# A decoder trunk in fp32 on one core: spare matmuls at the start, the first input chunk loaded first, and a last norm whose sums enter the root as its scale and bias

## The chip, the cores and the metric

The kernel runs on one core of a Trainium2 chip. The metric is device time in microseconds (us) of one execution; less is better. Three runs of the kernel before gave 1189.68, 1192.73 and 1192.95 us, a median of 1192.73. The profile and the trace come from a fourth, profiled execution.

A core has engines that run their own instruction streams and wait for each other by semaphores: TensorE (PE, with its weight loads as PEld), VectorE (DVE), ScalarE (ACT), GpSimd (POOL) and SyncE (SP). SP, POOL and ACT also start DMA transfers; each of these rows stands in the queue of the engine that issues it.

## What is computed

The input is x (512 tokens of 1024 numbers, float32). Two layers follow each other, an SGU mixer and a retention mixer, each with a SwiGLU feed-forward behind it; every block has an RMS norm in front and a residual add behind, and one RMS norm ends the trunk:

```python
def rmsnorm(x, g):
    xf = x.astype(jnp.float32)
    y = xf * lax.rsqrt(jnp.mean(xf * xf, axis=-1, keepdims=True) + EPS)
    return (y * g.astype(jnp.float32)).astype(x.dtype)
...
    h = x
    for i in range(DEPTH):
        hn = rmsnorm(h, mix_norm_g[i])
        j = i // N_MIXERS
        if i % N_MIXERS == 0:
            h = h + sgu_mixer(hn, sgu_w_in[j], sgu_w_s[j], sgu_b_s[j],
                              sgu_ln_g[j], sgu_ln_b[j], sgu_w_out[j])
        else:
            h = h + retention(hn, positions, ret_w_in[j], ret_gn_g[j], ret_w_out[j])
        h = h + swiglu(rmsnorm(h, ffn_norm_g[i]), ffn_w_gu[i], ffn_w_down[i])
    return rmsnorm(h, final_norm_g)
```

The change touches two ends of this: the first products of the SGU mixer, those of the half `v` of `gelu(h @ w_in)`, and the last line.

## The kernel before

The tokens are worked on in four chunks (`NC`) of 128, the partitions of a tile. Every fp32 product is made of three products of fp32r halves: a matrix is split into a high half (a copy on ACT: `wh`, `XH`) and a low half (the difference, on DVE: `wl`, `XL`), and PE adds up wh·XH, wl·XH and wh·XL. Most of the large products after the first also use sums of blocks in the manner of Strassen (`seven`, L836); they fill the middle of the span and are not touched.

No instruction is issued where it stands in the code. A `Recorder` (L211) takes each call down as an operation with its engine, the tiles that it reads and writes, and an estimate of its duration (`record`, L285). `order_of` (L423) then plans: `deadlines` goes back from the end and gives each operation a latest time, `forward` (L462) goes through the time from the start and gives each engine, whenever it is free, the operation whose inputs are there and whose latest time is nearest; it also models the DMA queues, each with its issue time by engine (SP 450, POOL 1200, ACT 100 in the planner's units) and a landing time, and grants buffers. `emit` (L619) writes the operations in this order to the engines' streams. The order on an engine is then fixed: an instruction whose input is late holds up all that stand behind it on that engine. Since everything goes through the recorder, nearly all rows of the profile carry one line, L337, and are told apart by the names of their tiles.

The start (L1342 to L1367): the rows of the first norm's gain go through a DMA of POOL (`load_rows`), X's first chunk and the first weight (`wr_v`) come on SP, in halves of 128x512 that the planner has put in turn: weight, X, weight, X. `rows_to_cols` turns the gain rows by a small matmul into `mix_ps`, which DVE copies into `mix_cols`. `turn_in(c)` (L1193) turns chunk c by eight transposes on PE into `xT_in`; ACT makes the high half `XH_in` in eight pieces, scaled by `mix_cols`; DVE makes `xr_in` and from it the low half `XL_in`, in two halves each. `square_in` (the tile `xq`) sums the squares of a chunk, for chunk 0 on DVE and for the others on ACT. `natural_step` (L820) adds the three products of two blocks of 128 rows into `ps_v`. Five small matmuls on a tile of ones, `wake` (ten instructions in the trace), stand ahead of all that on PE. `ones`, `eps` and the identity are made on POOL. Behind the products of `v`'s first half PE does `gains_ps`, the turned gains of the later norms.

The end: the last down product writes into X by blocks (`into_x`, L1031), and for each half (j) of a chunk (c) the last norm follows: `chunk_norm` (L1137) squares the half on ACT with a sum (`sq_dn`), `with_gain` (L1304) multiplies it by the gain `g_fin` on DVE for all but chunk 1's second half, and with the second half the two sums are added (`ss_dn`). `norm_factor` (L1161) makes 1/sqrt from the sum with a root on ACT, a reciprocal on DVE and a refinement step of three rows on DVE (all `nf_dn`); `finish` (L1313) scales the halves (`o`) on ACT, or on DVE for chunk 1, and sends each with a DMA, chunk 0's on ACT's queue and the others on SP's. Chunk 1's second half is the last to be ready.

## Time and profile before

| | |
|---|---|
| median of three runs | 1192.73 us (1189.68 to 1192.95) |
| profiled execution, its own time | 1187.3 us |
| its span in the trace | 1185.6 us |
| PE busy | 1168.7 us in 7494 matmul rows |
| ACT busy, DVE busy | 691.1 us, 999.5 us |
| first matmul (`wake`), first product of `ps_v` | 2.33 us, 8.77 us |
| PE's last matmul starts, last row on DVE starts | 1177.70 us, 1181.71 us |

The span is what the trace covers, 1.7 us less than the profiled execution's own time; the runs without a profile lie 2.4 to 5.7 us above that. A row of the timeline has a start and a duration in us, the engine, the line, the operation with output and inputs, the tile's shape, a count where equal rows follow each other, and in brackets how long the engine stood idle before it and what ended that. Matmuls are pipelined: the distance from one start to the next tells PE's pace better than a row's duration.

### The profile page before, as it was taken

To read this page: it belongs to the slowest core of one execution; us is meant where nothing else is said; L and a number is where in the kernel's file an instruction comes from. 1 tells how busy PE (TensorE), PEld (TensorE's weight loads), DVE (VectorE), ACT (ScalarE), POOL (GpSimd) and SP (SyncE) were. 2 spreads that over 40 slices of the span, in tenths; PEclk is the share of its full clock that TensorE was granted. 3 is DMA by queue.
4 is the path that set the end of the run, shared out by engine and by line. 5 is a ranking of instruction groups with operands and counts; after the bars stand their busy time and mean duration, and the time that the engine had idled before them with its cause. 6 is when DMAs were issued, how large, how long until landed. Compare 5 with 4: busy or idle time off the path is not lost.

```text
span 1185.6 us, 18730 instructions
## 1 busy us (share of the span) xinstructions
PE 1168.7 (99%) x7494; PEld 1064.7 (90%) x7494; DVE 999.5 (84%) x1168; ACT 691.1 (58%) x870; POOL 180.3 (15%) x159
## 2 busy tenths in 40 slices
PE   8999999999999999999999999999999999999997
PEld 6899899989999988888989898888899989999986
DVE  7998999897779799998968678899988896665895
ACT  7445776455443567756656575577675555435474
POOL 1002121211100120221111011220211111001220
PEclk9999999999999999999999999999999999999999
DMA  9349989798855888879667688698897798668891
GB/s 331 98 123 207 317 183 219 169 244 199 218 155 143 204 177 273 195 173 238 161 175 175 157 204 202 169 172 262 226 213 178 182 240 206 174 174 234 187 231 72
DMA packets 132808, 232.99 MB, mean 197 GB/s; under 512 B 7624, under 2 KB 32240, under 8 KB 132720
## 3 DMA queue, kind: packets, MB, share of 16 engines
q1 hardware_dynamic: 90928, 156.52, 40.4%
q0 software_dynamic: 41504, 74.74, 37.7%
q8 instruction: 59, 0.97, 0.3%
q10 hardware_dynamic: 288, 0.52, 0.1%
q14 instruction: 29, 0.24, 0.1%
HBM read 228.61 MB, written 2.10 MB: 195 GB/s over the span
## 4 chain that ended last, share of the span: by engine, by line
PE 89%; DVE 6%; DMA 3%; ACT 1%; issue 1%; DVEq 0%; ACTq 0%; SPq 0%; POOLq 0%
PE X_gu L337 21%; PE Y_gu L337 10%; PE X_dn L337 8%; PE X_vg L337 7%; PE Z_gu L337 5%; PE Y_dn L337 4%; PE X_qk L337 4%; PE Y_vg L337 4%; PE ps_v L337 4%; PE X_ro L337 3%; PE pv L337 2%; PE Y_qk L337 2%; PE X_so L337 2%; PE Y_ro L337 2%; PE Z_dn L337 2%; PE X_u L337 1%
## 5 line engine op out<-in xcount | busy, mean ns | idle before, releaser
L337 ACT ACTIVATE wh_gu_P<-wr_gu_P 128x1024 fp32r<-128x1024 f32 x132 | 137.4, 1055 | 124.2 <-DVE wr_gu_P L337 39.9
L337 DVE TENSOR_TENSOR wl_gu_P<-wr_gu_P,wh_gu_P 128x1024 fp32r<-128x1024 f32 x132 | 159.5, 1221 | 48.4 <-ACT wh_gu_P L337 39.9
L337 POOL DMA_DIRECT2D wr_gu_P<-in_ffn_w_gu x50 | 60.8, 1245 | 380.1 <-DVE wl_gu_P L337 161.3
L337 ACT ACTIVATE wh_dn_P<-wr_dn_P 128x1024 fp32r<-128x1024 f32 (+1 forms) x72 | 69.2, 981 | 44.4 <-PE Y_gu L337 9.5
L337 DVE TENSOR_TENSOR wl_dn_P<-wr_dn_P,wh_dn_P 128x1024 fp32r<-128x1024 f32 (+1 forms) x72 | 80.2, 1130 | 7.1 <-ACT wh_dn_P L337 6.5
L337 POOL DMA_DIRECT2D wr_dn_P<-in_ffn_w_down x40 | 46.4, 1202 | 173.0 <-DMA wr_dn_P<-in_ffn_w_down 66.9
L337 DVE TENSOR_TENSOR wl_vg_P<-wr_vg_P,wh_vg_P 128x1024 fp32r<-128x1024 f32 x48 | 57.4, 1219 | 8.7 <-ACT wh_vg_P L337 7.6
L337 ACT ACTIVATE wh_vg_P<-wr_vg_P 128x1024 fp32r<-128x1024 f32 x48 | 49.1, 1059 | 18.0 <-DMA wr_vg_P<-in_ret_w_in 9.5
L337 POOL DMA_DIRECT2D wr_vg_P<-in_ret_w_in x26 | 32.2, 1321 | 135.9 <-DVE wl_vg_P L337 61.4
L337 PE MATMUL X_gu<-xP3h_f,wh_gu_P 128*128 128x256 f32 x176 | 50.3, 286 | 0.0
L337 PE MATMUL X_gu<-xP5h_f,wh_gu_P 128*128 128x256 f32 x176 | 49.9, 284 | 0.3 <-ACT u L337 0.3
L337 PE MATMUL Z_gu<-XH_f,wh_gu_P 128*128 128x256 f32 x176 | 50.0, 284 | 0.0
L337 PE MATMUL X_gu<-XH_f,wh_gu_P 128*128 128x256 f32 x176 | 49.9, 284 | 0.0
L337 PE MATMUL Y_gu<-xP7l_f,wh_gu_P 128*128 128x256 f32 x176 | 49.8, 283 | 0.0
L337 PE MATMUL X_gu<-xP6h_f,wh_gu_P 128*128 128x256 f32 x176 | 49.8, 283 | 0.0
L337 PE MATMUL X_gu<-xP6l_f,wh_gu_P 128*128 128x256 f32 x176 | 49.8, 283 | 0.0
L337 PE MATMUL X_gu<-xP6h_f,wl_gu_P 128*128 128x256 f32 x176 | 49.8, 283 | 0.0
L337 PE MATMUL Y_gu<-XL_f,wh_gu_Q 128*128 128x256 f32 x176 | 49.8, 283 | 0.0
L337 PE MATMUL Y_gu<-XH_f,wl_gu_Q 128*128 128x256 f32 x176 | 49.8, 283 | 0.0
L337 PE MATMUL Y_gu<-xP7h_f,wl_gu_P 128*128 128x256 f32 x176 | 49.8, 283 | 0.0
L337 PE MATMUL Y_gu<-xP7h_f,wh_gu_P 128*128 128x256 f32 x176 | 49.8, 283 | 0.0
L337 PE MATMUL Y_gu<-XH_f,wh_gu_Q 128*128 128x256 f32 x176 | 49.8, 283 | 0.0
(675 smaller groups left out, 4377.8 us busy)
## 6 DMA issues: line engine op xcount, KB each, us to landing
wr_gu_P<-in_ffn_w_gu SPq DMA_DIRECT2D x110, 512.0 KB, 5.4
wr_gu_P<-in_ffn_w_gu POOLq DMA_DIRECT2D x50, 512.0 KB, 7.8
wr_dn_P<-in_ffn_w_down SPq DMA_DIRECT2D x50, 512.0 KB, 5.3
wr_vg_P<-in_ret_w_in SPq DMA_DIRECT2D x40, 512.0 KB, 5.2
wr_dn_P<-in_ffn_w_down POOLq DMA_DIRECT2D x33, 512.0 KB, 7.5
wr_vg_P<-in_ret_w_in POOLq DMA_DIRECT2D x26, 512.0 KB, 7.8
wr_qk_P<-in_ret_w_in SPq DMA_DIRECT2D x20, 512.0 KB, 4.7
wr_ro_P<-in_ret_w_out SPq DMA_DIRECT2D x20, 512.0 KB, 4.8
```

Of the source, the lines that this page charges most:

```text
L337: return fn(*[real_of(a) for a in args], **{k: real_of(a) for k, a in kwargs.items()})
```

## The change

At the start, 60 spare matmuls are offered to the planner: products of `onesr` with itself, 128 columns wide, into `vps[1]`, the second `ps_v` tile, which is overwritten later. `forward` puts one on PE wherever PE would have nothing to do between 2500 and 14000 of its time units, as long as that tile has not had its first product, and counts it with 120 units before 7000 and 60 behind; 52 are used. Before 7000 all PE operations count double. X's first chunk and the gain's rows get an earlier place (`rec.ahead`), so that X's two loads stand ahead of the first weight's on SP. Loads granted early are counted late by 600 instead of 1500, and a DMA issue on ACT costs 450 instead of 100. `ones` and `eps` are set on DVE.

At the end, the first half's sum becomes `base` = sum/D + EPS at once, and when the second half's sum s is there, the root is taken as sqrt(s/D + base) with 1/D as the activation's scale and `base` as its bias, without an add of the two sums (`norm_parts`). It gives r (the reciprocal of the root) and u (the refinement's factor) apart; chunk 1 is scaled by both at once, the others by their product z on ACT. All halves are multiplied by the gain beforehand, chunk 1's second half too; a chunk's second half is scaled and sent first, and only one of the eight outputs, chunk 1's first half, goes out on ACT's queue.

The order on PE at the start of the program, before the change (`xT_in` are the transposes of a chunk, `ps_v` the products):

```order
L337 MATMUL wake<-ones 128x128 x5
L337 MATMUL mix_ps<-ident,mix_rows 128x8
L337 MATMUL xT_in_123<-ident,X 128x128 x8
L337 MATMUL ps_v_0_147<-wh_v_0_115,XH_in 128x512
L337 MATMUL ps_v_0_147<-wl_v_0_126,XH_in 128x512
L337 MATMUL xT_in_158<-ident,X 128x128 x8
L337 MATMUL ps_v_0_147<-wh_v_0_115,XL_in 128x512
L337 MATMUL ps_v_0_147<-wh_v_0_115,XH_in 128x512
```

The same place of PE in the changed kernel, from behind `wake` (L1397 are the spares; `ps_v_1` is the tile that they write):

```order
L343 MATMUL mix_ps<-ident,mix_rows 128x8
L343 MATMUL xT_in_127<-ident,X 128x128 x5
L1397 MATMUL ps_v_1_110<-onesr 128x128 x5
L343 MATMUL ps_v_0_159<-wh_v_0_145,XH_in 128x512
L1397 MATMUL ps_v_1_110<-onesr 128x128
L343 MATMUL ps_v_0_159<-wl_v_0_155,XH_in 128x512
L1397 MATMUL ps_v_1_110<-onesr 128x128 x22
L343 MATMUL xT_in_201<-ident,X 128x128 x4
L1397 MATMUL ps_v_1_110<-onesr 128x128 x6
L343 MATMUL xT_in_201<-ident,X 128x128 x4
L1397 MATMUL ps_v_1_110<-onesr 128x128 x2
L343 MATMUL ps_v_0_159<-wh_v_0_145,XL_in 128x512
```

Twelve more spares, and three transposes of chunk 0, stand between `wake` and these rows. The transposes of chunk 0 now stand ahead of and behind `mix_ps`, and 30 spares with the eight transposes of chunk 1 lie between the second product of `ps_v` and the first with `XL_in`.

The order on ACT at the start, before (`wh_v` is the high half of a weight, `XH_in` that of a chunk):

```order
L337 ACTIVATE wh_v_0_115<-wr_v_0_80 128x512 x2
L337 ACTIVATE XH_in<-xT_in_123,mix_cols 128x128 x8
L337 ACTIVATE wh_v_1_161<-wr_v_1_100 128x1024
L337 ACTIVATE XH_in<-xT_in_158,mix_cols 128x128 x8
L337 ACTIVATE wh_v_2_198<-wr_v_2_109 128x1024
L337 ACTIVATE xq_209,ss_140<-X 128x1024
L337 ACTIVATE wh_v_3_225<-wr_v_3_117 128x1024
```

And the same place of ACT in the changed kernel:

```order
L343 ACTIVATE wh_v_0_145<-wr_v_0_94 128x512
L343 ACTIVATE XH_in<-xT_in_127,mix_cols 128x128 x8
L343 ACTIVATE wh_v_0_145<-wr_v_0_94 128x512
L343 ACTIVATE wh_v_1_194<-wr_v_1_104 128x1024
L343 ACTIVATE xq_216,ss_141<-X 128x1024
L343 ACTIVATE XH_in<-xT_in_201,mix_cols 128x128 x8
L343 ACTIVATE wh_v_2_254<-wr_v_2_117 128x1024
```

The second half of the first weight has moved behind `XH_in` of chunk 0, and the squares of a chunk (`xq`) have moved ahead of `XH_in` of chunk 1.

The order on DVE at the end of the program, before, from the last add into X on (`nf_dn_1_1` are the small tiles of chunk 1's norm, `o` the outputs):

```order
L337 TENSOR_TENSOR X<-X,W_dn_1_11799 128x512
L337 TENSOR_TENSOR ss_dn_1_11781<-ss_dn_1_11654 128x1
L337 TENSOR_SCALAR nf_dn_1_1_11875<-ss_dn_1_11781 128x1
L337 RECIPROCAL nf_dn_1_1_11877<-nf_dn_1_1_11873 128x1
L337 SCALAR_TENSOR_TENSOR nf_dn_1_1_11879<-nf_dn_1_1_11877,nf_dn_1_1_11875 128x1
L337 TENSOR_SCALAR nf_dn_1_1_11881<-nf_dn_1_1_11879 128x1
L337 TENSOR_TENSOR nf_dn_1_1_11883<-nf_dn_1_1_11881,nf_dn_1_1_11877 128x1
L337 TENSOR_SCALAR o_0_11722<-o_0_11722,nf_dn_1_1_11883 128x512
L337 SCALAR_TENSOR_TENSOR o_1_11886<-X,nf_dn_1_1_11883,g_fin 128x512
```

And the end of DVE's stream in the changed kernel:

```order
L343 TENSOR_TENSOR X<-X,W_dn_1_11858 128x512
L343 TENSOR_TENSOR o_1_11928<-X,g_fin 128x512
L343 TENSOR_SCALAR nf_dn_1_1_11932<-ss_dn_1_11704,nf_dn_1_1_11788 128x1
L343 RECIPROCAL nf_dn_1_1_11934<-nf_dn_1_1_11930 128x1
L343 SCALAR_TENSOR_TENSOR nf_dn_1_1_11936<-nf_dn_1_1_11934,nf_dn_1_1_11932 128x1
L343 TENSOR_SCALAR nf_dn_1_1_11938<-nf_dn_1_1_11936 128x1
L343 TENSOR_SCALAR o_1_11928<-o_1_11928,nf_dn_1_1_11938,nf_dn_1_1_11934 128x512
L343 TENSOR_SCALAR o_0_11791<-o_0_11791,nf_dn_1_1_11938,nf_dn_1_1_11934 128x512
```

The add of the sums and the last small multiply are gone, the product of the last half with the gain has moved ahead of the norm's small rows, and both scalings take two of them.

The diff, cut where it only passes the list of spares on:

```diff
--- before.py
+++ after.py
@@ -32,6 +32,7 @@
 SUM = 7
 N_GEN = 39
 N_TMP = 5
+SPARES = 60
 SO = ("P1", "P7", "P6", "Q4", "P5", "P2", "P3")
 UO = ("P1", "P7", "P6", "P2", "Q4", "P5", "P3")
 U_DMA = ("P7",)
...
@@ -253,6 +254,11 @@
         self.ops.append(op)
         return op
 
+    def spare(self, call, tile):
+        op = Op()
+        op.engine, op.call, op.what, op.tiles, op.n = "PE", call, "spare", [tile], 0
+        self.spares.append(op)
+
     def issue_after(self, ins):
         return nullcontext()
 
@@ -305,7 +311,7 @@
     if name == "dma_start":
         kind = "add" if "accum_op" in kwargs else "load" if writes else "store"
         size = n * 4 * (writes or reads)[0].shape[0]
-        busy = {"SP": 450, "POOL": 1200, "ACT": 100}[engine]
+        busy = {"SP": 450, "POOL": 1200, "ACT": 450}[engine]
         took = busy
         slow = max(60, size * (SERVE_ADD if kind == "add" else SERVE) // 524288)
     elif name == "transpose":
@@ -353,6 +359,12 @@
 BOTH = 0.95
 LATE = 1500
 ROUNDS = 1
+FILL_FROM = 2500
+FILL_TO = 14000
+WARM = 7000
+SPARE = 120
+EARLY_LOADS = 4000
+LATE_FIRST = 600
 SURE = 2000
 EARLY = False
 POOL_DATA = 640
@@ -431,21 +443,21 @@
-        end = forward(ops)
+        end, used = forward(ops, rec.spares)
...
-    return sorted(ops, key=lambda o: (o.start, o.n))
+    return sorted(ops + used, key=lambda o: (o.start, o.n))
...
@@ -512,8 +524,9 @@
             kind = min((k for k in lane if lane[k]), key=lambda k: lane[k][0][1] / rate(k))
             op = lane[kind].pop(0)[0]
             op.end = now
-            started(op, now + LATE)
-            post(now + LATE, op)
+            late = LATE if op.start > EARLY_LOADS else LATE_FIRST
+            started(op, now + late)
+            post(now + late, op)
         left = [max(0, q[0][1]) / rate(kind) for kind, q in lane.items() if q]
         if left:
             version += 1
@@ -531,6 +544,13 @@
     grant()
     finished = 0
     soon = {"DVE": [], "ACT": []}
+    used, left = [], spares[::-1]
+
+    def may_fill():
+        if not left or not FILL_FROM <= now < FILL_TO:
+            return False
+        t = left[-1].tiles[0]
+        return t.granted is not None and t.first.start is None
 
     def started(op, end):
         for q in op.after:
@@ -588,6 +608,13 @@
                             cost = o.late + (3 * TABLE if o.table and o.table != table else 0)
                             if op is None or (cost, o.n) < best:
                                 op, best = o, (cost, o.n)
+                if op is None and e == "PE" and may_fill():
+                    op = left.pop()
+                    used.append(op)
+                    op.start = now
+                    busy_until[e] = now + (SPARE if now < WARM else SPARE // 2)
+                    post(busy_until[e], None)
+                    continue
                 if op is None or e in soon and not op.kind and better(e, op):
                     break
                 queue[e].remove(op)
@@ -596,7 +623,7 @@
                     if q.left == 0:
                         queue["PE"].append(q)
                 op.start = now
-                held = op.busy
+                held = op.busy * 2 if e == "PE" and now < WARM else op.busy
                 if op.table and op.table != table:
                     table = op.table
                     held += TABLE
...
@@ -679,9 +706,9 @@
     ident = const.tile([P, P], F32, name="ident")
     rec.add("POOL", lambda: make_identity(rec.real, ident.realize()), [], [ident.view()], "identity", 600, 600)
     ones = const.tile([P, P], F32, name="ones")
-    nc.gpsimd.memset(ones, 1.0)
+    nc.vector.memset(ones, 1.0)
     eps = const.tile([P, 1], F32, name="eps")
-    nc.gpsimd.memset(eps, EPS)
+    nc.vector.memset(eps, EPS)
     onesr = const.tile([P, P], F32R, name="onesr")
     nc.vector.tensor_copy(onesr, ones)
     nc.scalar.activation(const.tile([P, 1], F32, name="first"), ones[:, 0:1], AF.Gelu_apprx_tanh)
@@ -1137,7 +1164,7 @@
     def chunk_norm(name, ready, half=None):
 
 
-        halves_of = [0] * NC
+        halves_of, first_half = [0] * NC, [None] * NC
         ss = small.tile([P, NC], F32, tag="ss", name=f"ss_{name}")
         part = small.tile([P, 2 * NC], F32, tag="ss0", name=f"ss0_{name}")
 
@@ -1153,10 +1180,27 @@
                     half(c, j)
                 halves_of[c] += 1
                 if halves_of[c] == 1:
+                    if half:
+                        base = small.tile([P, 1], F32, tag="nf16", name=f"nf6_{name}_{c}", bufs=4)
+                        nc.vector.tensor_scalar(base, both[:, j:j + 1], 1.0 / D, EPS, ALU.mult, ALU.add)
+                        first_half[c] = base
+                    return
+                if half:
+                    ready(c, norm_parts(both[:, j:j + 1], first_half[c], f"{name}_{c}"))
                     return
                 nc.vector.tensor_tensor(ss[:, c:c + 1], both[:, 0:1], both[:, 1:2], ALU.add)
             ready(c, norm_factor(ss[:, c:c + 1], D, f"{name}_{c}"))
         return norm
+
+    def norm_parts(ss, base, name):
+
+        a, root, r, t, u = (small.tile([P, 1], F32, tag=f"nf1{i}", name=f"nf{i}_{name}", bufs=4) for i in range(5))
+        nc.scalar.activation(root, ss, AF.Sqrt, scale=1.0 / D, bias=base)
+        nc.vector.tensor_scalar(a, ss, 1.0 / D, base, ALU.mult, ALU.add)
+        nc.vector.reciprocal(r, root)
+        nc.vector.scalar_tensor_tensor(t, r, a, r, ALU.mult, ALU.mult)
+        nc.vector.tensor_scalar(u, t, -0.5, 1.5, ALU.mult, ALU.add)
+        return r, u
 
     def norm_factor(ss, n, name):
 
@@ -1305,24 +1349,22 @@
 
         if not fin:
             fin.append(gain_tile("g_fin", fin_g[None, :]))
-        if (c, j) != (1, 1):
-            o = gained[c, j] = G(f"o{c}_{j}")[:, 0, :]
-            js = slice(j * T, (j + 1) * T)
-            nc.vector.tensor_tensor(o, X[:, c, js], fin[0][:, js], ALU.mult)
-
-    def finish(c, r):
-        for j in range(2):
-            js = slice(j * T, (j + 1) * T)
-            if (c, j) in gained:
-                o = gained[c, j]
-                if c == 1:
-                    nc.vector.tensor_scalar(o, o, r, None, ALU.mult)
-                else:
-                    nc.scalar.activation(o, o, AF.Copy, scale=r)
+        o = gained[c, j] = G(f"o{c}_{j}")[:, 0, :]
+        js = slice(j * T, (j + 1) * T)
+        nc.vector.tensor_tensor(o, X[:, c, js], fin[0][:, js], ALU.mult)
+
+    def finish(c, ru):
+        r, u = ru
+        if c != 1:
+            z = small.tile([P, 1], F32, tag="nf15", name=f"nf5_end_{c}", bufs=4)
+            nc.vector.tensor_tensor(z, u, r, ALU.mult)
+        for j in (1, 0):
+            o = gained[c, j]
+            if c == 1:
+                nc.vector.tensor_scalar(o, o, u, r, ALU.mult, ALU.mult)
             else:
-                o = TMP(f"o{c}_{j}")
-                nc.vector.scalar_tensor_tensor(o, X[:, c, js], r, fin[0][:, js], ALU.mult, ALU.mult)
-            (nc.scalar if c == 0 else nc.sync).dma_start(out[c * P:(c + 1) * P, js], o)
+                nc.scalar.activation(o, o, AF.Copy, scale=z)
+            (nc.scalar if (c, j) == (1, 0) else nc.sync).dma_start(out[c * P:(c + 1) * P, j * T:(j + 1) * T], o)
 
 
     ss2 = small.tile([P, NC], F32, tag="ss2", name="ss2", bufs=1)
@@ -1339,8 +1381,10 @@
         else:
             nc.scalar.activation(sq, X[:, c, :], AF.Square, accum_out=ss2[:, c:c + 1])
 
+    rec.ahead = 3000
     load_rows(nc.gpsimd, "mix0", mix_g[0:1])
     load_x(0)
+    rec.ahead = 0
     v0w = [None] * NC
     wr = G("wr_v0_0")
     for a in range(2):
@@ -1348,6 +1392,12 @@
     mix0 = rows_to_cols("mix0")
     turn_in(0)
     vps = [PS(f"ps_v0_{i}") for i in range(2)]
+
+    def keep_warm():
+        rec.real.tensor.matmul(vps[1][:, 0, 0:P].realize(), onesr.view().realize(), onesr.view().realize(), start=True, stop=True)
+
+    for _ in range(SPARES):
+        rec.spare(keep_warm, vps[1])
     for i in range(NC):
         if i > 0:
             wr = fetch_tile(f"v0_{i}", w_in, 2 * i, 2, ((D, T),))
```

More of the change, by code (lines that the diff above doesn't have):

```diff
@@ L215, in __init__ @@
         self.tc, self.real = tc, tc.nc
-        self.ops, self.held, self.ahead = [], {}, 0
+        self.ops, self.held, self.ahead, self.spares = [], {}, 0, []
         for attr in ENGINE_OF:
@@ L433, in order_of @@
         deadlines(ops, total)
-        end = forward(ops)
+        end, used = forward(ops, rec.spares)
         if best is None or end < best[0]:
-            best = end, [(o.start, o.end, o.late) for o in ops], [(t, t.granted, t.when) for o in ops for t in o.new]
+            best = end, [(o.start, o.end, o.late) for o in ops], [(t, t.granted, t.when) for o in ops for t in o.new], used
         total = end
@@ L440, in order_of @@
                 op.late = op.start
-    end, times, places = best
+    end, times, places, used = best
     for op, (op.start, op.end, op.late) in zip(ops, times):
@@ L459, in deadlines, with forward @@
     backward(ops, lazy, total, gap)
-def forward(ops):
+def forward(ops, spares):
     import heapq
@@ L615, in forward @@
                            f"{ {k[1]: (len(slots[k]), len(w)) for k, w in waiting.items() if w} }")
-    return now
+    return now, used
 def emit(rec):
```

## The prediction

> **What bounds the kernel now.** I read the page first (busy times, then the chain that ended last), then PE's waits behind the start, then the timeline of the first 36 us and of the last 8.
>
> ```profile
> PE 1168.7 (99%) x7494; PEld 1064.7 (90%) x7494; DVE 999.5 (84%) x1168; ACT 691.1 (58%) x870; POOL 180.3 (15%) x159
> PE 89%; DVE 6%; DMA 3%; ACT 1%; issue 1%; DVEq 0%; ACTq 0%; SPq 0%; POOLq 0%
> PE X_qk L337 <- ACT xP6h_r L337: 1.5, 1, 1.5
> ...
> PE X_gu L337 <- ACT u L337: 0.3, 1, 0.3
> ```
>
> PE works 99% of the 1185.6 us span and is 89% of the chain. The three rows below the chain are the first and the last of all seven waits that PE has after 12 us: 5.2 us together, none of them on a DMA. So almost any time that PE gains or loses at the start is passed on to the end, and only the start and the tail behind PE's last matmul can move. Those are the two places that the change touches; the order of the middle is the same but for two neighbouring weight loads on SP.
>
> The start, from the timeline (start, duration, what; in brackets the idle time before and its releaser):
>
> ```profile
> 0.81 0.39 SPq L337 DMA_DIRECT2D wr_v<-in_sgu_w_in  x1
> 2.04 0.24 POOL L337 MEMSET ones<- 128x128 f32 x1
> 2.33 2.50 PE L337 MATMUL wake<-ones 128*128 128x128 f32 x10 [2.33 <-POOL ones L337]
> 5.21 0.63 ACT L337 ACTIVATE wh_v<-wr_v 128x512 fp32r<-128x512 f32 x1 [2.70 <-DMA wr_v<-in_sgu_w_in]
> 6.12 0.24 PE L337 MATMUL mix_ps<-ident,mix_rows 8*128 8x8 f32 x1 [1.28 <-DMA mix_rows<-in_mix_norm_g]
> 6.40 0.17 DVE L337 COPY mix_cols<-mix_ps 128x8 f32<-128x8 f32 x1 [3.86 <-PE mix_ps L337]
> 6.54 0.63 ACT L337 ACTIVATE wh_v<-wr_v 128x512 fp32r<-128x512 f32 x1 [0.70 <-DMA wr_v<-in_sgu_w_in]
> 7.20 0.72 PEld L337 LDWEIGHTS xT_in<-ident,X 128*128 128x128 f32 x4 [0.19 <-DMA X<-in_x]
> 7.82 1.22 DVE L337 SCALAR_TENSOR_TENSOR xq<-X 128x1024 f32<-128x1024 f32 x1
> 8.35 2.18 ACT L337 ACTIVATE XH_in<-xT_in,mix_cols 128x128 fp32r<-128x128 f32 x8 [1.18 <-PE xT_in L337]
> 8.77 0.80 PE L337 MATMUL ps_v<-wh_v,XH_in 128*128 128x512 f32 x1 [0.46 <-ACT XH_in L337]
> 9.79 1.88 PE L337 MATMUL xT_in<-ident,X 128*128 128x128 f32 x8
> 11.29 0.69 DVE L337 TENSOR_TENSOR XL_in<-xr_in,XH_in 128x512 fp32r<-128x512 f32 x1
> 12.04 0.50 PE L337 MATMUL ps_v<-wh_v,XL_in 128*128 128x512 f32 x1 [0.36 <-DVE XL_in L337]
> 12.37 0.40 PE L337 MATMUL ps_v<-wh_v,XH_in 128*128 128x512 f32 x1
> 14.90 0.60 PE L337 MATMUL xT_in<-ident,X 128*128 128x128 f32 x4
> 15.39 0.50 PE L337 MATMUL ps_v<-wh_v,XL_in 128*128 128x512 f32 x1
> 21.46 1.03 PE L337 MATMUL xT_in<-ident,X 128*128 128x128 f32 x8
> 22.25 0.47 PE L337 MATMUL ps_v<-wh_v,XH_in 128*128 128x512 f32 x1
> 35.63 0.25 PE L337 MATMUL gains_ps<-ident,gains_rows 32*128 32x32 f32 x1
> ```
>
> Two things are to be seen. The first four transfers land one after the other, 0.65 us apart: first at 5.2, third at 6.54, fourth at 7.2, so the second at about 5.9. And PE has two speeds: eight transposes take 1.88 us at 9.79 (0.235 each), and 0.79 from 21.46 to 22.25 (0.1 each); a 512-column product takes 0.228 (the chain's row of 22.50, below). It became fast shortly before 12.04: 2.9 to 3.3 us after the work that began, with hardly a break, at 8.77, or 5.9 us after that of 6.12.
>
> **The start, changed.** X's two halves come first and land at 5.2 and 5.9; the memset of ones moves from POOL, where a DMA and its start-up stood ahead of it until 2.04, to DVE, where it is the first instruction: from 0.81, when SP begins, 0.24 later wake can begin, at 1.05 instead of 2.33. eps, the second, is wanted by nothing near the start. PE then has work without a break: wake, 12 spares, transposes. By 2.9 to 3.3 us of unbroken work it is fast at 4 to 4.4; by 5.9 at 7. I take the first, as the break at 4.83 to 6.12 in the old start speaks for a fresh count. The gains do not follow from X alone, though. mix_ps still waits for its rows until 6.12 (its DMA stays on POOL), and ACT's first wh_v now stands ahead of XH_in and takes the third landing: 6.54 + 0.63 = 7.2. So XH_in begins at 7.2 instead of 8.35 and its last input of chunk 0 (xr_in, half a wl_v, XL_in) is there at about 11.35 rather than 11.98 (8.35 to 11.98 is 3.6; plus 0.6 for the wl_v now between, less overlap).
>
> That 0.6 us is not what PE sees. DVE holds mix_cols (to 6.6), xq (1.22) and the first wl_v (0.69, the row of XL_in has the same size) ahead of the second product: it starts at 8.5 and ends at 8.7. Behind it the order puts 22 + 6 + 2 spares and the 8 transposes of chunk 1 ahead of the product with XL_in. What does a spare cost? It is a 128-column fp32r product, and the trace has such ones late in the retention layer:
>
> ```profile
> 609.60 0.26 PE L337 MATMUL sc<-q1h,k1h 128*128 128x128 f32 x1
> ...
> 610.26 0.44 PE L337 MATMUL Y_vg<-wh_vg_Q,XL_r 128*128 128x512 f32 x1
> 22.50 13.20 PE ps_v L337 x58
> 170.60 5.76 PE Z_gu L337 x48
> ```
>
> Six of them stand from 609.60 to 610.26: 0.11 each. (The last two rows, from the chain, give 0.228 for 512 columns and 0.12 for 256; a line through them would make 128 columns 0.066.) I take 0.11, the row of the same size. Then the XL_in product starts at 8.7 + 30 x 0.11 + 8 x 0.1 = 12.8, against 12.04: **+0.8**. The spares that were to fill idle time outlast it by 1.4 us, since the data is there at 11.35. Behind it stand four more spares between chunk 2's transposes, +0.4; against that, the slow first product of 12.04 (0.33 to the next, 0.1 over) and some 0.2 of the 14.90 to 15.39 stretch (four transposes in 0.49, where 21.46 gives 0.4, and a slow product behind) may go. Start: 0.8 + 0.4 - 0.3 = **+0.9**.
>
> Bounds: with spares at 0.066 the product with XL_in waits for its data at 11.35, the later chunks' XL_in (XH_in of chunk 1 starts no sooner than 11.74 now, as the second wh_v, wh_v_1 and xq_1 stand ahead of it on ACT, 11.71 before) hold part of the gain, and -0.6 is left. With PE slow until 7, twelve spares at 0.235 end at 6.4 instead of 5.0, the transposes and with them XH_in come some 0.5 later: +1.6. With PE slow until 10.8 it is +2.3.
>
> The Trainium skill bears on both numbers. TensorE: Matmul & The Clock Gate, section "Back-to-back issue gap", gives about 81 ns for a pair of weight load and 128-column matmul; the six in this trace took 110, and by 81 the start would come out near -0.3. The same page, section "Part 1: The HAM clock gate", speaks of a free-running window of about 3.4 us of activity, which would make PE fast somewhere from 4.5 to 7.9; the granted clock of the profile's windows reads 1.00 from the first stretch on and doesn't show it, the pace of the transposes does.
>
> **The tail, changed.** From the timeline of the end; the last two rows are from the views by tile (min/median/max ns, and DMA us to landing of the outs):
>
> ```profile
> 1178.13 0.69 DVE L337 TENSOR_TENSOR X<-X,W_dn 128x512 f32<-128x512 f32 x1 [0.97 <-PE W_dn L337]
> 1178.21 0.95 ACTq L337 DMA_DIRECT2D out<-o  x2
> 1179.20 0.63 ACT L337 ACTIVATE sq_dn<-X 128x512 f32<-128x512 f32 x1 [0.42 <-DVE X L337]
> 1179.96 0.16 DVE L337 TENSOR_TENSOR ss_dn<-ss_dn 128x1 f32<-128x1 f32 x1 [1.14 <-ACT sq_dn L337]
> 1180.15 0.29 ACT L337 ACTIVATE nf_dn<-ss_dn,eps 128x1 f32<-128x1 f32 x1 [0.23 <-DVE ss_dn L337]
> 1181.12 0.16 DVE L337 TENSOR_TENSOR nf_dn<-nf_dn,nf_dn 128x1 f32<-128x1 f32 x1
> 1181.31 0.48 DVE L337 TENSOR_SCALAR o<-o,nf_dn 128x512 f32<-128x512 f32 x1
> 1181.71 0.74 DVE L337 SCALAR_TENSOR_TENSOR o<-X,nf_dn,g_fin 128x512 f32<-128x512 f32 x1
> L337 DVE TENSOR_SCALAR v<-v,mv,ry_ln x8: 539/540/545, 64.8 to 68.0; 128x512 f32<-128x512 f32 x8
> DMA to landing us min/median/max: 2.0/2.1/2.2
> ```
>
> X is ready at 1178.82, but the square starts at 1179.20, as ACT first issues two outs (1178.21, 0.95). Those move to SP: -0.33. The ss add goes (1179.96 to 1180.15): -0.19; the multiply of 1181.12 goes: -0.19. The first scaling takes two pointers, as the v row does: 0.54, starts following at 0.46 instead of 0.40, +0.06; the last one 0.54 instead of 0.74: -0.20. Sum **-0.85** at the last result. It is then sent on ACT's queue; landings range from 2.0 to 2.2, so -0.65 to -0.85 at the end, and I take -0.8. The new product of X with the gain (0.69, the size of X<-X,W_dn) lies on DVE beside the square and the reading of its sum (1179.20 to 1179.96); without that cover it would cost 0.69. The two outs on SP stand behind outs that have gone by then, and the last comes 2 us later. The base of chunk 1 is one tiny row (0.16) long before.
>
> **Sum.** +0.9 - 0.8 = +0.1 us. The profiled execution of 1187.3 us (span 1185.6) becomes 1187.4; it lies 5.4 under the median of the three runs, 1192.73, to which I add the same: **1192.8**.
>
> **Rivals.**
> - *Spares are cheap.* If 128 columns cost 0.066 to 0.08, PE reaches XL_in with its data and the earlier X counts: start -0.6 to -0.3, with the tail -1.4 to -1.1: 1191.4. For it: the line through 256 and 512 columns, and that all spares load one and the same tile; against it: the six at 0.11.
> - *Slower: PE stays slow longer.* The mechanism is the pace of 0.235 for the first spares and chunk 0's transposes; it decides if PE is fast only after 6 us (5.0 + the 1.1 that mix_ps leaves). At 7 the start costs +1.6, at 10.8 +2.3: net +0.8 to +1.5, 1193.5 to 1194.2; I take 1193.8. For it: 5.9 us from 6.12 to 12.04 in the old start; that PE never becomes fast early, the far end, is also the case in which the spares don't do what they are for.
> - *The tail doesn't land.* The last out on ACT's queue, or a square that still waits, keeps 0.5 of the 0.8: net +0.6, 1193.3.
>
> **Chances.** Forecast 0.45, cheap spares 0.22, slow PE 0.23, tail 0.06, others 0.04. None of the cases reaches 0.3% (3.6 us, about what a measurement of this kernel can tell from no change); what does is the scatter of the runs, 1189.68 to 1192.95, of which a median of few may take either end: 3.05 below the median, 0.2 above. So the low end is 1189.2, the forecast at the low run less half of what the cheap spares give, and the high end 1194.4, the slow case with 0.2. Faster by over 0.3%: 0.10, within: 0.84, slower: 0.06.
>
> **What would show it.** PE's wake at 1.05 and its transposes of chunk 0 at 0.1 each (fast) or 0.235 (slow); the spacing of the 22 spares, 0.11; the product with XL_in at 12.8 with no wait, its data at 11.35; gains_ps behind the ps_v products 0.9 later than now (35.63); the square directly behind X, and 2.8 us from X's end to the last result's end, where it is 3.6. I am wrong if the gains_ps row comes earlier than now, or if a wait on DMA shows up behind 36 us.

## The result, and the profile after

| | before | changed |
|---|---|---|
| median of 19 runs each | 1192.73 us (1186.9 to 1194.35) | 1199.42 us (1193.23 to 1202.03) |
| ratio | | 1.0061, 95% interval 1.0046 to 1.0076 |
| profiled execution, its span | 1187.3, 1185.6 us | 1196.61, 1194.9 us |
| `gains_ps` starts | 35.63 us | 42.80 us |
| PE's last matmul starts | 1177.70 us | 1187.69 us |
| last matmul to the end of the span | 7.9 us | 7.2 us |

The change makes the kernel 6.7 us slower at the median; 1192.8 was forecast, in a range of 1189.2 to 1194.4. In the two profiles the spans differ by 9.3 us: 7.2 at the start, 2.8 more between `gains_ps` and the last matmul, and 0.7 less behind it.

The start of the changed kernel, from PE's timeline (start and duration in us; a row with xN has N equal instructions, and the distance to the next row, by N, is PE's pace):

```profile
1.13 2.50 PE L343 MATMUL wake<-ones 128*128 128x128 f32 x10 [1.13 <-DVE eps L343]
3.69 2.82 PE L1397 MATMUL ps_v<-onesr 128*128 128x128 f32 x12
6.31 0.86 PE L343 MATMUL xT_in<-ident,X 128*128 128x128 f32 x3
7.10 0.27 PE L343 MATMUL mix_ps<-ident,mix_rows 8*128 8x8 f32 x1
7.30 1.33 PE L343 MATMUL xT_in<-ident,X 128*128 128x128 f32 x5
8.28 1.31 PE L1397 MATMUL ps_v<-onesr 128*128 128x128 f32 x5
9.39 0.73 PE L343 MATMUL ps_v<-wh_v,XH_in 128*128 128x512 f32 x1
9.92 0.31 PE L1397 MATMUL ps_v<-onesr 128*128 128x128 f32 x1
10.03 0.73 PE L343 MATMUL ps_v<-wl_v,XH_in 128*128 128x512 f32 x1
10.56 4.79 PE L1397 MATMUL ps_v<-onesr 128*128 128x128 f32 x22
15.15 1.08 PE L343 MATMUL xT_in<-ident,X 128*128 128x128 f32 x4
15.88 1.52 PE L1397 MATMUL ps_v<-onesr 128*128 128x128 f32 x6
17.19 1.08 PE L343 MATMUL xT_in<-ident,X 128*128 128x128 f32 x4
17.92 0.67 PE L1397 MATMUL ps_v<-onesr 128*128 128x128 f32 x2
18.39 0.73 PE L343 MATMUL ps_v<-wh_v,XL_in 128*128 128x512 f32 x1
18.92 0.63 PE L343 MATMUL ps_v<-wh_v,XH_in 128*128 128x512 f32 x1
19.35 0.63 PE L343 MATMUL ps_v<-wl_v,XH_in 128*128 128x512 f32 x1
19.77 0.45 PE L343 MATMUL ps_v<-wh_v,XL_in 128*128 128x512 f32 x1
20.06 0.40 PE L343 MATMUL ps_v<-wh_v,XH_in 128*128 128x512 f32 x1
...
42.80 0.24 PE L343 MATMUL gains_ps<-ident,gains_rows 32*128 32x32 f32 x1
```

From 1.13 on PE hardly pauses, and still it is slow for 18 us and more: the 22 spares take 4.59 us (10.56 to 15.15), 0.209 each, and a product of 512 columns 0.43 (18.92 to 19.35). It turns fast at 19.9, 1.5 us after the 512-column products begin to follow one another. The trace's own record of the granted clock begins at that moment: its first entry is the rise to full, at 19.88 here and at 11.51 before the change. The product with `XL_in` starts at 18.39, 6.3 us later than before the change; its data is there from 12.76 on (DVE's `XL_in`, 12.08 and 0.68 long). The other 0.8 us of the shift are the first products behind it, still slow, and the four spares of chunk 2, less some shorter waits.

The tail, from the timeline of the changed kernel, answers to the one in the prediction:

```profile
1188.12 0.69 DVE L343 TENSOR_TENSOR X<-X,W_dn 128x512 f32<-128x512 f32 x1 [1.55 <-PE W_dn L343]
1188.84 0.63 ACT L343 ACTIVATE sq_dn<-X 128x512 f32<-128x512 f32 x1
1188.84 0.69 DVE L343 TENSOR_TENSOR o<-X,g_fin 128x512 f32<-128x512 f32 x1
1189.59 0.29 ACT L343 ACTIVATE nf_dn<-ss_dn,nf_dn 128x1 f32<-128x1 f32 x1
1190.56 1.00 DVE L343 TENSOR_SCALAR o<-o,nf_dn,nf_dn 128x512 f32<-128x512 f32 x2
```

The square starts directly behind X, the product with the gain lies beside it, and from X's end (1188.81) to the last result's end (1191.56) it is 2.75 us instead of 3.63.

### The profile page after: what moved, and what is told of

Read it like the earlier page. It is cut to its first block, busy times and chain, and to the rows that moved or that the text cites. A ratio compares the mean times of both kernels' runs of the same rounds, so it can differ in the third digit from the quotient of the medians.

```text
span 1194.9 us, 18837 instructions
## 1 busy us (share of the span) xinstructions
PE 1179.6 (99%) x7546; PEld 1076.0 (90%) x7546; DVE 999.3 (84%) x1170; ACT 690.4 (58%) x870; POOL 180.1 (15%) x157
## 4 chain that ended last, share of the span: by engine, by line
PE 74%; DVE 4%; DMA 3%; ACT 1%; issue 1%; DVEq 0%; ACTq 0%
PE X_gu L343 19%; PE Y_gu L343 10%; PE X_dn L343 7%; PE X_vg L343 7%; PE Z_gu L343 4%; PE X_qk L343 4%; PE Y_vg L343 4%; PE Y_dn L343 3%; PE X_ro L343 3%; PE pv L343 2%; PE Y_qk L343 2%; PE Y_ro L343 2%; PE Z_dn L343 2%; PE Z_vg L343 1%; DMA wr_dn_P<-in_ffn_w_down 1%; PE sc L343 1%
## 5 line engine op out<-in xcount | busy, mean ns | idle before, releaser
L343 ACT ACTIVATE wh_dn_P<-wr_dn_P 128x1024 fp32r<-128x1024 f32 (+1 forms) x72 | 69.3, 981 | 45.3 <-DMA wr_dn_P<-in_ffn_w_down 10.9
```

The source lines that it names most:

```text
L343: return fn(*[real_of(a) for a in args], **{k: real_of(a) for k, a in kwargs.items()})
```

## The experiments

Each edit is of the changed kernel, unless it says otherwise. "Mean clock" is the granted clock over a whole run, which each timed run reports. The ratio compares a run with runs of the kernel before made beside it, with its 95% interval in brackets; it is not the quotient of two medians. The medians of those runs beside it went from 1191.7 to 1193.4 us between experiments, so medians of different experiments are comparable to some 2 us only.

**1. No spares (no_spares).** X first, the memsets, ACT's new order and the new tail stay.

```diff
-SPARES = 60
+SPARES = 0
```

> The changed kernel without its spares; X first, the moved memsets, ACT's new order and the new last norm stay. Theory A (a stretch of some 3.4 us has to be filled with work that keeps the array busy, and a 128-column spare, 0.214 us at the slow pace where 512 columns take 0.43, leaves it idle half of the time): PE is fast by about 9 to 13 us as before the change, the product with XL_in starts at 12 to 13, gains_ps at 35 to 36.5; 1190.5 to 1192.5, 7 to 9 under the changed kernel. Rival B (the spares cost their own 52 x 0.214 us but don't decide when PE becomes fast, which came at 19.8 us): XL_in at about 12.8 but the pace slow until 19 or so, gains_ps near 39; 1195 to 1196. Rival C (the spares are innocent, the order of X and of ACT is what costs): XL_in near 18, about 1199.

Measured: 1193.09 us, ratio to the kernel before 0.9996 (0.998 to 1.0012); 6.3 under the changed kernel. `XL_in`'s product starts at 11.84, `gains_ps` at 37.02; PE turns fast at 15.7, behind 5.8 us of work without a break (from 9.93 on). So it is the spares that cost, not the order of X and of ACT: C is out. B's 19 us is out as well. A is right about what costs, but not in its numbers: PE turned fast later than the 9 to 13 us that it gave, and `gains_ps` and the time lie above its ranges.

**2. Only the first twelve (early_spares).**

```diff
-FILL_TO = 14000
+FILL_TO = 5600
```

> Only the first 12 spares, those before X's first chunk has landed, stay (the filling ends at 5600 of the planner's units instead of 14000). Theory A: they end near 6.3 us as before, when X could begin, so they cost at most 0.6; PE is fast at 9 to 14; 1191 to 1193. Rival B: 12 x 0.214 less than all 52, so 40 x 0.214 = 8 us of PE time less, but fast only at 19: 1195 to 1196. Rival C: about 1199.

Measured: 1193.17 us, 1.0009 (0.9986 to 1.0031). PE's timeline: the twelve end at 6.3, `XL_in`'s product starts at 12.82 at the fast pace, `gains_ps` at 36.70. The time is 0.2 above A's range. The first twelve neither help nor do much harm (`gains_ps` comes 1.1 later than before the change, and without any spares 1.4); the 40 behind them are what the changed kernel pays for.

**3. Wide spares (wide_spares).** 512 columns for each spare, the ones read four times over.

```diff
-SPARE = 120
+SPARE = 450
...
-        rec.real.tensor.matmul(vps[1][:, 0, 0:P].realize(), onesr.view().realize(), onesr.view().realize(), start=True, stop=True)
+        rec.real.tensor.matmul(vps[1][:, 0, :].realize(), onesr.view().realize(), onesr[:, None, :].to_broadcast([P, 4, P]).realize(), start=True, stop=True)
```

> Spares of 512 columns (the ones read four times over) in the place of 128, 0.45 in the planner's count; 16 of them are used, 9 behind the second product and ahead of the first with XL_in. Theory A: they fill the array at the slow pace (0.43 us for 512 columns), so PE is fast at the end of the first or second full stretch of 3.4 us behind 1.1, that is 4.5 to 8; the transposes of chunk 0 take 0.1 to 0.2 each, XL_in starts at 11.3 to 12.5, gains_ps at 34.9 to 36.2; 1190.5 to 1192. Rival B: PE stays slow until 19 whatever fills it, 16 x 0.43 = 6.9 us of spares: XL_in at 17 or later, 1198 to 1200. Rival C: about 1199.

Measured: 1191.91 us, 0.9991 (0.9974 to 1.0008), 7.5 under the changed kernel. PE's timeline:

```profile
3.69 1.56 PE L1397 MATMUL ps_v<-onesr 128*128 128x512 f32 x4
5.08 0.27 PE L343 MATMUL xT_in<-ident,X 128*128 128x128 f32 x1
5.28 0.22 PE L343 MATMUL mix_ps<-ident,mix_rows 8*128 8x8 f32 x1
5.44 0.98 PE L343 MATMUL xT_in<-ident,X 128*128 128x128 f32 x7
...
9.25 1.32 PE L1397 MATMUL ps_v<-onesr 128*128 128x512 f32 x5
...
12.24 0.43 PE L343 MATMUL ps_v<-wh_v,XL_in 128*128 128x512 f32 x1
```

Seven transposes take 0.74 us (5.44 to 6.18), 0.1 each, and five spares 1.16: PE is fast from about 4.5 on. That is theory A's number, and B, for which it doesn't matter what fills PE, is out. The start gains nothing by it, though: `gains_ps` comes at 36.03, where it came at 35.63 before the change, since the first product waits 1.55 us for ACT's `XH_in`.

The spare's price also changes how many spares the planner uses: 16 here, 26 and 12 in runs 6 and 7, in place of 52. Up to 4.5 us the orders differ only in the form of the spares behind `wake`, so their number isn't what decides there.

**4. The new tail alone (tail_alone).** The kernel before with `chunk_norm`, `norm_parts`, `with_gain` and `finish` of the change.

> The kernel before with the new last norm alone. All theories: the start as before; from X's last add to the last result 2.75 us instead of 3.63, time 0.7 to 0.9 under the kernel before, 1191.9 against 1192.7. If the 2.8 us that the changed kernel loses between gains_ps and the last matmul came from the new tail's g_fin or outputs, they would show here: 1194.5.

Measured: 1191.25 us, 0.9989 (0.997 to 1.0008); `gains_ps` at 35.64, the last matmul at 1176.79 and the span's end at 1184.0, 7.2 us later, as in the changed kernel. The tail's share lands, and the 2.8 us of the middle don't come from it: the stretch from `gains_ps` to the last matmul takes 1141.2 here and 1142.1 in the kernel before. By time alone 1 us is not told from none.

**5. The changed kernel again (after_again).**

> The changed kernel once more, for a second look at its start. Theory A (a stretch of 3.4 us counts only if the array is busy most of it, and these stretches lie on a grid that falls differently in each run): PE is fast nowhere before the first 512-column products that follow one another, so between 18.4 and 22 us, and the 30 spares between the second product and XL_in take 0.21 each again; gains_ps at 42 to 43.5. Rival B (19.8 us was one bad run): fast at 10 to 15, gains_ps at 36 to 39.

Measured, one run: 1196.08 us. `XL_in`'s product at 18.39, the 22 spares from 10.56 to 15.15 again, PE fast at 20.5, `gains_ps` at 43.11. The late clock is no accident of one run.

**6. Spares of 256 columns (mid_spares).** As 3, with half the columns and 240 as the planner's count.

> Spares of 256 columns. Theory A: at the slow pace 256 columns keep the array busy 0.213 of some 0.24 us, so these spares count like wide ones: PE fast at 4.5 to 9, gains_ps at 35.5 to 36.5, time 1191 to 1193. Rival D (what matters is not the share but that a spare is one 512-column instruction, or any weight load in between counts as idle): slow until the products follow one another, 18 or later, 1197 to 1200.

Measured: 1192.38 us, 0.9992 (0.9974 to 1.001); PE fast at 4.6, `gains_ps` at 35.28.

**7. Spares of 128 columns in plain fp32 (fp32_spares).**

```diff
-SPARE = 120
+SPARE = 500
...
-        rec.real.tensor.matmul(vps[1][:, 0, 0:P].realize(), onesr.view().realize(), onesr.view().realize(), start=True, stop=True)
+        rec.real.tensor.matmul(vps[1][:, 0, 0:P].realize(), ones.view().realize(), ones.view().realize(), start=True, stop=True)
```

> Spares of 128 columns again, but of plain fp32 like wake (two rows of 0.25 us each at the slow pace). Theory A: they keep the array busy most of the time although they are only 128 columns wide: PE fast at 4.5 to 9, gains_ps at 35.5 to 37, 1191 to 1193. Rival D: narrow is narrow, PE slow until 18 or later, 1197 to 1200.

Measured: 1190.33 us, 0.9983 (0.9965 to 1.0002); PE fast at 4.7, `XL_in`'s product at 11.46 and `gains_ps` at 35.01, the earliest of all. PE's timeline (a spare is two rows):

```profile
3.69 1.39 PE L1397 MATMUL ps_v<-ones 128*128 128x128 f32 x6
4.91 0.38 PE L343 MATMUL xT_in<-ident,X 128*128 128x128 f32 x2
...
11.46 0.47 PE L343 MATMUL ps_v<-wh_v,XL_in 128*128 128x512 f32 x1
```

The spare has the 128 columns of the change's and brings the clock up: D, by which narrow is narrow, is out. So the form of the spare decides; why is argued, not shown. Theory A has it that PE must spend most of its time in the array. By the pace of 512 columns, 0.43 us, 128 columns would take 0.107 of a spare's 0.209, about half, and 256 columns 0.215, while a spare of 256 takes hardly longer than the narrow one (two in 0.43, 4.07 to 4.50 in run 6). This share is an estimate from the paces, and for the plain fp32 spare no row gives it at all.

**8. Filling a stall in the middle (fill_qk).** The runs' mean clock and a fall of the granted clock near 505 us (below) pointed to a second place. tail_alone, with ten wide spares ahead of the first product into `Y_qk`:

```diff
+    at = next(i for i, o in enumerate(order) if o.engine == "PE" and o.what == "matmul Y_qk0")
...
+    order[at:at] = spares
```

> tail_alone with ten wide spares (2.3 us at the fast pace) on PE just ahead of the first product into Y_qk, where PE otherwise idles 1.5 to 5.4 us and where two of the four profiles show the granted clock at half for 3.4 and 6.8 us. Theory A: the clock falls there when a stretch of the grid is mostly idle; filled, it doesn't fall, or less often: the runs with a mean clock of 0.997 or less (7 to 8 of 12 in tail_alone) become rare, the median goes from 1191.3 to 1186 to 1188.5. Rival E (the fall at 507 us comes from something else, such as the load before it): the mixture stays, median 1191 to 1193.

Measured: 1189.97 us, 0.9971 (0.9955 to 0.9986). The profile shows that the filling missed its aim: the spares had to wait themselves, 2.52 us for ACT's `XH_r`, and stood behind the gap instead of in it. The median lies between the forecasts of A and E. Mean clocks are 0.997 to 0.999, where tail_alone had 0.994 to 0.999, and the clock still fell in the profile, for one stretch. That the idle time is the cause is likely from this, but not shown.

**9. The kernel before, again (before_again).**

> The kernel before once more. If the fall of the granted clock near 505 us and the late transfer of a weight (wr_vg) that ACT waits for there belong to both kernels, most runs of it have them (26 of 29 had a mean clock of 0.997 or less): 1191 to 1195 with ACT's wait for wr_vg at 4 to 5 us and PE's waits in front of Y_qk and X_qk at 4 us or more in total. If only the changed kernel has them: 1187, waits as in the first profile (1.5).

Measured, one run: 1186.24 us, mean clock 0.999, ACT's wait for `wr_vg` 1.21 us, PE's wait for `xP6h_r` 0.9, no fall of the clock. A miss: this run was one of the minority again (7 of the 23 runs beside it had 0.998 or more). So no profile shows the kernel before with the long waits; what there is on them comes from run 10.

**10. One row of ACT moved (unblock).** tail_alone, with the high half of one weight behind `xP6h_r` in the order, and what depends on it:

```diff
-    return sorted(ops, key=lambda o: (o.start, o.n))
+    return later(sorted(ops, key=lambda o: (o.start, o.n)), "activation wh_vg0_P7_0_2", "activation xP6h_r")
```

The reason was in the profiles of runs 1 and 3. ACT's timeline in wide_spares, where PE waited 3.6 us for `xP7h_r` and 1.8 for `xP6h_r`:

```profile
496.78 1.04 ACT L343 ACTIVATE wh_qk_P<-wr_qk_P 128x1024 fp32r<-128x1024 f32 x1
503.01 1.06 ACT L343 ACTIVATE wh_vg_P<-wr_vg_P 128x1024 fp32r<-128x1024 f32 x1 [5.19 <-DMA wr_vg_P<-in_ret_w_in]
503.97 1.07 ACT L343 ACTIVATE xr_r<-xT_r 128x512 f32<-128x512 f32 x2
504.93 1.03 ACT L343 ACTIVATE XH_r<-xT_r 128x1024 fp32r<-128x1024 f32 x1
505.84 1.06 ACT L343 ACTIVATE xP7h_r<-xP_r 128x1024 fp32r<-128x1024 f32 x1
```

ACT waited 5.19 us for one weight's transfer, and the activations that PE waited for stood behind that row though they didn't need it. The windows of the same run (length, PE busy and its instructions, the granted clock, then the DMA engines' share and GB/s):

```profile
502.00:504.00 2.00, 1.40 (x7) 1.00 0.61 71
504.00:506.00 2.00, 0.00 (x0) 1.00 1.07 190
506.00:508.00 2.00, 0.58 (x1) 0.57 0.94 257
508.00:510.00 2.00, 0.65 (x3) 0.50 1.12 222
510.00:512.00 2.00, 2.00 (x11) 0.50 0.30 52
512.00:514.00 2.00, 2.00 (x15) 0.73 0.00 0
```

PE idles, the clock falls to half, and it stays there for some 3 us in which PE is busy again. By the trace's record the fall lasts 6.83 us here, and 3.41 us in no_spares, mid_spares and fill_qk.

> tail_alone with one row of ACT moved: the high half of the weight vg0_P7_0_2, whose transfer came 1.0 to 5.2 us late in the profiles so far, stands behind xP6h_r instead of ahead of xr_r of chunk 1 (the low half on DVE already stood behind it). Theory F (this row holds up xr_r, XH_r and xP7h_r on ACT, these hold up PE in front of Y_qk and X_qk, and a stretch that PE idles through halves the clock): PE's waits for xP7h_r and xP6h_r fall below 1.5 us in all, the clock stays up, 10 or more of 12 runs at 0.998 or more, median 1185 to 1187. Rival G (the late transfer stops the work behind it all the same, since PE needs the weight 6 us later): 1190 to 1192 and the mixture stays.

Measured: 1186.69 us (1184.56 to 1188.26), 0.9961 (0.9945 to 0.9977); all 12 runs have a mean clock of 0.998 or more. Against tail_alone, which has the same tail, the median is 4.6 lower. ACT's timeline of unblock:

```profile
495.31 1.09 ACT L337 ACTIVATE xr_r<-xT_r 128x512 f32<-128x512 f32 x2 [1.35 <-PE xT_r L337]
496.28 1.04 ACT L337 ACTIVATE XH_r<-xT_r 128x1024 fp32r<-128x1024 f32 x1
497.51 1.06 ACT L337 ACTIVATE xP7h_r<-xP_r 128x1024 fp32r<-128x1024 f32 x1 [0.20 <-DVE xP_r L337]
...
500.87 1.05 ACT L337 ACTIVATE wh_vg_P<-wr_vg_P 128x1024 fp32r<-128x1024 f32 x1
```

The weight's row has no wait where it stands now, and PE's for `xP6h_r` is 0.2 us. F holds, G is out. The mean clock alone wouldn't do as evidence: mid_spares' profile has 0.998 and a fall all the same. The times bear it out, all 12 of them at 1188.26 or less. For the kernel before, whose order this is otherwise, it makes the same stall likely in most of its runs: 16 of the 23 beside it had a mean clock of 0.997 or less and a median of 1193.0, the other 7 one of 1185.9. That isn't shown, as both profiles of that kernel are of the faster kind.

**11. Both (fp32_unblock).** fp32_spares with the same row moved.

> The changed kernel with spares of plain fp32 and with the same row of ACT moved. Theory A and F together: start as in fp32_spares (gains_ps at 35.0 to 35.5), no fall of the clock at 505 us; 0.2 to 0.7 under unblock, median 1184.5 to 1186.5. Rival (the start's gain is not passed on): equal to unblock or above.

Measured: 1186.43 us (1185.12 to 1188.44), 0.9972 (0.9952 to 0.9991); `gains_ps` at 35.20, where unblock has 35.32. Not told from unblock: 0.1 us at the start, where the profiles gave 0.6 between fp32_spares and the old start (35.01 and 35.64). Both versions are faster than the kernel before, with intervals that stay below 1.

**12. The changed kernel with the row moved (after_unblock).**

> The changed kernel as it is, narrow spares and all, with the one row of ACT moved as in unblock. If the start is all that the spares cost, this differs from unblock, which has the old start and the same tail, by the shift of gains_ps alone: 7.2 to 7.8 us, so 1193.5 to 1195 with nearly all runs at a mean clock of 0.998 or more. If the late start also costs something in the middle (transfers that collide otherwise, waits at the first products of a layer), it is 1196 or more.

Measured: 1194.49 us, 7.8 above unblock; 9 of 12 runs at 0.998 or more. Of the 12, nine lie from 1194.19 to 1197.63, the other three at 1188.71, 1189.08 and 1190.87. In the profiled one `gains_ps` starts at 42.40, 7.1 later than in unblock. The medians agree with the theory by which the start is all that the spares cost, but the profiles don't: the last matmul starts 10.7 us later than in unblock (1186.51 and 1175.84), so 3.6 us came in the middle. The largest part is one wait of PE, in unblock and then in after_unblock, where ACT's `xP7h_r` now waited for DVE:

```profile
PE X_qk L337 <- ACT xP6h_r L337: 0.2, 1, 0.2
PE X_qk L343 <- ACT xP6h_r L343: 2.0, 1, 2.0
507.84 1.06 ACT L343 ACTIVATE xP7h_r<-xP_r 128x1024 fp32r<-128x1024 f32 x1 [1.67 <-DVE xP_r L343]
```

It is not one run's accident. From `gains_ps` to the last matmul the three profiles with all 52 narrow spares take 1144.0 to 1144.9 us, and the seven others in which the clock doesn't fall take 1140.5 to 1142.6. Why a late start brings longer waits in the middle stays open. And once in a while PE seems to turn fast early all the same, by the three short times; no profile shows such a run.

## Why the prediction was wrong

**What bounds it** was right in that PE's time at the start is passed on to the end: none of the 7.2 us was made up for. But the prediction put the middle at nothing because its order is the same, and in the profiles the middle grew, by 2.8 us from before to the changed kernel and by 3.6 from run 10 to run 12.

**The tail** was right in its size and its parts: -0.85 was forecast at the last result and -0.88 came, -0.65 to -0.85 at the end and -0.7 came.

**The start** was forecast at +0.9 and came at +7.2. The step that failed is the one that took PE as fast "by 2.9 to 3.3 us of unbroken work", at 4 to 4.4. PE did work with hardly a break from 1.13, and was slow until 19.9 and 20.5. What decided there was what PE worked on, and not only the breaks, from which I had argued in the old start: with 512 columns, 256 columns or plain fp32 in the same places it was fast at 4.5 to 4.7, and at 6.0 in run 11. I counted a 128-column fp32r product as work like any other. Nor do 2.9 to 3.3 us without a break suffice with other work: no_spares took 5.8.

Two terms hung on that step. The price of a spare, 0.11, came from a row of the same size but at the fast pace; at the slow pace it was 0.209, and the 30 spares of the sum took 6.4 us instead of 3.3. (The four spares that ran fast, in chunk 2, took 0.12 each: there the row was right.) And `mix_ps` didn't start at 6.12 when its rows were there, but at 7.10, behind twelve slow spares and three slow transposes; `XH_in` began at 8.67 instead of 7.2 and the second product at 10.03 instead of 8.5. Together with that product (0.3 us longer) and the eight transposes (1.5 instead of 0.8) this makes the whole way from 12.8 to 18.39: 1.5 + 0.3 + 3.1 + 0.7.

The slower rival was the right mechanism, with 0.23 of the chances, and too short: it let PE be slow until 10.8 at most and charged +2.3. At its own pace of 0.235, the 30 spares alone would have been 30 x (0.235 - 0.11) = 3.8 us above the sum, and as long as they run, PE need not become fast. (That pace was read from a row's duration; from start to start the slow transposes took 0.21, 9.79 to 11.28 for seven of them.) The bound should have been the slow pace up to the first 512-column products, wherever the order puts them; with the rows measured since, that comes to some +7.

**The cheap rival** was off in its upper end too, which changed nothing: with a spare at 0.08 the sum's own terms give -0.1 at the start, not -0.3, and the -0.3 worked out beside it from 0.081 is -0.1 as well.

The Trainium skill's page TensorE: Matmul & The Clock Gate, section "Part 1: The HAM clock gate", has a free-running window of about 3.4 us and calls the warm-up a budget of time, not of matmuls. The runs agree with the first: in the traces' record, the stretches between two changes of the clock are 3.413 us or whole multiples of it (6.827 is 2, 491.519 is 144, 1170.772 is 343), wherever they begin (PE fast at 4.5 to 6.0 with the three other spares, 10.9 to 12.5 in the old start). They limit the second: 18 us of work, over half of it narrow spares, didn't use the budget up.

**The spread of the runs** was taken as scatter. At least in part it has a cause, the stall of run 10. Both profiles compared above are of faster runs, before by 5.4 us under its median and the changed kernel by 2.8, and so they differ by 9.3 where the medians differ by 6.7. The 2.8 us of the middle are mostly PE's waits: 7.2 us after the first 12 us in the changed kernel against 5.2 (2.0 instead of 1.5 for `xP6h_r`, 1.3 instead of 0.5 for X in front of `X_dn`).

## What to carry to other kernels

Filling an idle TensorE brought its clock up early here only with some forms of filler, and even then nothing clear of noise was gained, since the products behind waited for their data. Check the pace of the filler itself at the slow clock, and what stands behind it in the same queue when it is slow. A price from a row holds only at the clock of that row. Where runs of one program spread over more than half a per cent, read each run's mean clock first: here most of the spread went when one row was moved that stood ahead of work that didn't need it, and that was worth more (some 4 to 5 us at the median) than anything that the change was about.

## What the runs showed of the hardware that I had not expected

- Work of which more than half was 128-column fp32r products left PE at half speed for 18 to 19 us in all three profiles that have them throughout (fast at 19.9, 20.5 and 18.9); spares of 512 or 256 columns, or of 128 in plain fp32, brought it up at 4.5 to 6.0 (four profiles).
- The granted clock in the windows reads 1.00 from the first stretch on, also where the pace shows half speed: the trace's record of it begins with the first rise (19.88 in the changed kernel). At the start the pace has to be read.
- PE's waits for `xP7h_r` and `xP6h_r` near 505 us that add up to 4.4 us or more (no_spares 2.4 and 2.0, mid_spares 2.6 and 2.0, wide_spares 3.6 and 1.8 us) went with half speed for 3.4 to 6.8 us behind; in the other profiles they add up to 2.6 us or less and the clock stayed up, but for fill_qk, where one wait of 2.5 us went with 3.4 us at half speed.
- ACT waited from 1.0 to 5.2 us for the same transfer of a weight, in programs with the same order there. Why stays open.
